# A decoder trunk in fp32 on one core: the first modulation partly as raw fp32 products on TensorE, and four weight units loaded as wide rows

## Chip, core and metric

The kernel runs on one core of one Trainium2 chip. The metric is the device time of one launch in microseconds (us), and the kernel before takes a median of 2716.3 us over three runs. The engines are named as the profile names them: PE is TensorE (PEld its weight loads), DVE is VectorE, ACT is ScalarE, POOL is GpSimd, and SP issues nearly all transfers (DMAs).

## What is computed

Two decoder layers on one sequence of 1024 rows with 1024 columns. Each layer has a token mixer (a gated spatial MLP in layer 0, dilated attention in layer 1) and a dense MLP, and each of these four sub-layers is modulated by a vector c: a shift, a scale and a gate come out of a product of silu(c) with its own weights ada_w.

```python
def ada_mod(c, w, b):
    m = jax.nn.silu(c) @ w + b
    shift, scale, gate = jnp.split(m, 3, axis=-1)
    return shift[:, None, :], scale[:, None, :], 1.0 + gate[:, None, :]

def mixer_a(h, w_in, b_in, vn_g, vn_b, w_s, b_s, w_out):
    uv = jax.nn.gelu(h @ w_in + b_in)
    u, v = jnp.split(uv, 2, axis=-1)
    v = layer_norm(v, vn_g, vn_b)
    ...                                   # z: v mixed over rows within chunks of 128
    return (u * z) @ w_out

# layer i
shift, scale, gate = ada_mod(c, ada_w[i, 0], ada_b[i, 0])
h = x * (1.0 + scale) + shift
y = mixer_a(h, ...)                       # layer 1: mixer_b
x = layer_norm(ALPHA * x + gate * y, ln_g[i, 0], ln_b[i, 0])
...                                       # the same again with squared_relu_mlp
```

All data is fp32. ada_w of one sub-layer has 1024 rows (the index of c) and 3072 columns (shift, scale, gate).

## The kernel before

Every large product is made of three passes with fp32r operands: both factors are cut into a high part (a cast to fp32r) and a low part (the difference), by `split`, and PE adds high times high, high times low and low times high. Left factors stand as 128x128 weights, right factors stream 512 columns. The whole program is unrolled at build time into one fixed instruction list for each engine. A list scheduler sets the order on each engine, except where the code pins an instruction to program order (`tc.keep_in_program_order`). Each engine then runs its list strictly from the front and waits on semaphores.

The change lies in the first stage alone. Until the first modulation is known, no product of the model can run. In the kernel before the stage goes so:

- `c` and a part of ada_b are loaded into `rows_c`, transposed by PE (L79), and silu(c) stands as 8 columns of 128 in `silu_c`.
- `ada_steps` makes the modulation. For each of shift and scale (`part` 0 and 1) and each half of 512 columns (`h`), eight blocks of 128 rows of ada_w (`adaw`, 128x512, 256 KB, L122) are loaded and added up on DVE with silu(c) as the scalar of each partition: one TENSOR_SCALAR (L125) and seven SCALAR_TENSOR_TENSOR (L128) into `adaacc`. Then `adaacc` is split into `adahi` and `adalo`, and PE sums over the partitions: for each of four column blocks two products with `ones_r`, 128x2 (L162, L163, tile `psa`). DVE adds ada_b (L167). `mods(h)` runs shift and scale of one half side by side; up to ten `adaw` tiles are in flight.
- `build_hT` makes h transposed for rows 0 to 511, one block k of 128 columns at a time: four transposes on PE (`pst`, L221), scale and shift on ACT (L226, tile `h`), the cut into `hT` high and low (L102, L103). Blocks 0 to 3 need the first half of the modulation, blocks 4 to 7 the second.
- `v_sum` multiplies `hT` with the weights of v, eight units of 128 output columns. A unit's weights (`winv_raw`, 512 KB) come as 8 blocks of 128x128, that is in pieces of 512 bytes (L353); ACT casts the high part, and for the first four units POOL subtracts the low part (`winv_lo`, `v_unit(G)`). Blocks 0 to 3 are multiplied for units 0 to 3 between the two halves of the modulation, blocks 4 to 7 after them. `v_end` then applies the gelu (L475) and transposes back (`psvt`, L478).
- After that come rows 512 to 1023, the units 4 to 7 of v, the units of u, and the rest of the kernel. The modulations of the later sub-layers run in the background in small steps (`tick`), with the same `ada_steps`.

All loads of this stage stand in one queue on SP in program order. A load waits there until the buffer that it fills is free, and everything behind it waits with it.

## Time and profile before

| | |
|---|---|
| median of three runs | 2716.3 us (2712.53 to 2717.81) |
| the profiled execution's own time | 2717.79 us |
| its span (first to last instruction) | 2716.1 us |
| PE busy in the span | 2655.5 us (98%) |
| first product of a v unit starts (L470) | 25.81 us |
| last product of units 0 to 3 on rows 0 to 511 starts | 60.4 us |
| HBM traffic over the span | 185 GB/s |

A row of the profile's timeline gives the start in us from the span's start, the duration in us, engine, line, operation, output<-inputs, the count of like instructions that were merged, and in brackets how long the engine was idle before and what released it. Durations of merged rows run from the first start to the last end. A row of the table by stretches gives busy us and instruction counts for each engine, the clock that the throttle granted to PE, the DMA share and GB/s.

### The profile page before, as it was taken

The numbers are of one execution on the slowest core, as the hardware profiler recorded it, in microseconds if no ns is written. First come the engines' busy times: TensorE is split into PE (matmuls) and PEld (weight loads), VectorE is DVE, ScalarE is ACT, GpSimd is POOL, SyncE is SP. The second block draws the span as 40 slices with busy tenths as digits, with TensorE's granted clock in tenths as the row PEclk, the third lists the DMA queues.
The fourth block names the chain that finished last, engine by engine and source line by source line (L and its number), as shares of the span: only waits on it lengthen the run. The fifth ranks groups of instructions, "written<-read, shape, count | busy, mean of one in ns | idle before, by whom it ended". The sixth has DMA issues, their size and how long they took to land.

```text
span 2716.1 us, 37099 instructions
## 1 busy us (share of the span) xinstructions
PE 2655.5 (98%) x13242; PEld 2193.5 (81%) x13242; DVE 1993.0 (73%) x3610; ACT 1378.4 (51%) x2601; POOL 114.9 (4%) x193
## 2 busy tenths in 40 slices
PE   6999999999999999999999999999999999999998
PEld 5788887888788878888888888888887888878887
DVE  6787697777889778655647767777658966577877
ACT  3354375555444454433436666666645655544332
POOL 1000000000000001111111000000010000000000
PEclk9999999999999999999999999999999999999999
DMA  7534336667967745655475545554782654495562
GB/s 264 159 118 135 116 137 217 223 223 243 344 229 247 245 148 180 215 179 198 165 225 172 138 133 140 138 146 133 235 219 98 213 190 155 147 317 183 172 208 86
DMA packets 340781, 504.77 MB, mean 186 GB/s; under 512 B 51900, under 2 KB 177252, under 8 KB 340596
## 3 DMA queue, kind: packets, MB, share of 16 engines
q1 hardware_dynamic: 324212, 443.68, 51.5%
q0 software_dynamic: 16384, 58.73, 6.0%
q8 instruction: 104, 1.70, 0.3%
q14 instruction: 81, 0.66, 0.1%
HBM read 365.40 MB, written 136.92 MB: 185 GB/s over the span
## 4 chain that ended last, share of the span: by engine, by line
PE 76%; DVE 12%; DMA 6%; ACT 3%; issue 2%; SPq 0%; DVEq 0%; ACTq 0%
PE psd L957 22%; PE psv L1283 13%; PE psk L1384 6%; PE psq L1384 6%; PE psua L798 6%; DMA adaw<-in_ada_w_dram 3%; PE psd_wout L389 3%; PE pv L1553 3%; PE psuc L798 3%; PE psu L368 3%; PE sc L1473 3%; PE psv L470 2%; DVE adaacc L128 2%; DVE left L103 1%; PE pT L1526 1%
## 5 line engine op out<-in xcount | busy, mean ns | idle before, releaser
L798 PE MATMUL psua<-right,left 128*128 128x512 f32 x1536 | 364.8, 391 | 0.1
L957 PE MATMUL psd<-rhi,lhi 128*128 128x512 f32 x896 | 349.7, 390 | 3.0 <-ACT part L829 3.0
L957 PE MATMUL psd<-rlo,lhi 128*128 128x512 f32 x896 | 349.6, 390 | 0.2
L957 PE MATMUL psd<-rhi,llo 128*128 128x512 f32 x896 | 349.3, 390 | 0.0
L798 PEld LDWEIGHTS psua<-right,left 128*128 128x128 f32 x1536 | 288.3, 188 | 61.6 <-DVE right L103 1.2
L1495 ACT ACTIVATE p<-p,stat 128x128 f32<-128x128 f32 (+1 forms) x384 | 168.8, 441 | 96.8 <-DVE stat L1493 95.8
L957 PEld LDWEIGHTS psd<-rhi,lhi 128*128 128x128 f32 x896 | 168.6, 188 | 39.2 <-ACT part L829 3.9
L957 PEld LDWEIGHTS psd<-rlo,lhi 128*128 128x128 f32 x896 | 168.5, 188 | 35.9 <-DVE rlo L103 1.1
L957 PEld LDWEIGHTS psd<-rhi,llo 128*128 128x128 f32 x896 | 168.6, 188 | 34.9
L798 PE MATMUL psuc<-right,left 128*128 128x512 f32 x768 | 187.2, 390 | 0.0
L128 DVE SCALAR_TENSOR_TENSOR adaacc<-adaw,silu_c,adaacc 128x512 f32<-128x512 f32 x168 | 128.6, 775 | 59.6 <-DMA adaw<-in_ada_w_dram 59.0
L798 PEld LDWEIGHTS psuc<-right,left 128*128 128x128 f32 x768 | 143.6, 188 | 29.9 <-DVE right L103 0.2
L103 DVE TENSOR_TENSOR pTlo<-pT,pThi 128x512 fp32r<-128x512 f32 (+1 forms) x160 | 99.3, 621 | 75.9 <-ACT pThi L102 75.0
L103 DVE TENSOR_TENSOR left<-ws,left 128x512 fp32r<-128x512 f32 x128 | 87.9, 688 | 73.2 <-ACT left L102 71.3
L103 DVE TENSOR_TENSOR llo<-lraw,lhi 128x1024 fp32r<-128x1024 f32 x112 | 136.4, 1218 | 1.5 <-ACT lhi L102 1.5
L102 ACT CAST left<-ws 128x512 fp32r<-128x512 f32 x128 | 79.1, 620 | 104.5 <-DVE ws L719 92.0
L1384 PE MATMUL psk<-form_L,wqk_hi 128*128 128x512 f32 x384 | 126.9, 411 | 0.0
L1384 PE MATMUL psq<-form_L,wqk_hi 128*128 128x512 f32 x384 | 126.4, 410 | 0.0
L102 ACT CAST lhi<-lraw 128x1024 fp32r<-128x1024 f32 x112 | 117.3, 1047 | 9.3 <-PE psd L957 3.3
L1283 PE MATMUL psv<-vrhi,form_S 128*128 128x512 f32 x384 | 120.0, 391 | 1.3 <-DVE vpart L1249 0.8
L1493 DVE CUSTOM_DVE_ANT_0 p<-sc,bias 128x128 f32<-128x128 f32 (+1 forms) x384 | 113.7, 346 | 5.2 <-PE sc L1473 4.9
L102 ACT CAST pThi<-pT 128x512 fp32r<-128x512 f32 (+1 forms) x160 | 84.6, 530 | 60.4 <-PE pT L1526 43.3
(332 smaller groups left out, 6072.3 us busy)
## 6 DMA issues: line engine op xcount, KB each, us to landing
lraw<-forms SPq DMA_DIRECT2D x112, 512.0 KB
adaw<-in_ada_w_dram SPq DMA_DIRECT2D x192, 256.0 KB
up<-in_mlp_w_up_dram SPq DMA_DIRECT2D x64, 512.0 KB
forms<-s SPq DMA_DIRECT2D x128, 256.0 KB
rraw<-in_mlp_w_down_dram SPq DMA_DIRECT2D x64, 512.0 KB
forms<-part SPq DMA_DIRECT2D x96, 256.0 KB
v<-vs POOLq DMA_DIRECT2D x48, 512.0 KB, 3.7
vraw<-in_b_w_qkv_dram SPq DMA_DIRECT2D x42, 512.0 KB
```

The source lines that it names most:

```text
L102: first = A.copy(hi, src) if hi_engine is A else hi_engine.tensor_copy(hi, src)
L103: return first, lo_engine.tensor_tensor(lo, src, hi, op=ALU.subtract)
L128: ins = V.scalar_tensor_tensor(acc[:], raw[:], silu_c[:, k : k + 1], acc[:], ALU.mult, ALU.add)
L368: T.matmul(dst, s[a], m[b], start=(n == 0), stop=(n == last))
L389: T.matmul(p[:], stat[a][:, k, o : o + P], u[b][:, w], start=n == 0, stop=n == count - 1)
L798: T.matmul(acc, w[:, a, k, :], right[p][:, b, k, :], start=p in (1, 2, 5) and k + a + b == 0, stop=k == 3 and a == 1, skip_group_check=True)
L957: ins = T.matmul(sums[kind, m][:], l[a][:, k, m * P : (m + 1) * P], r[b][:, k, :], start=p in (1, 5, 2, 3) and kp + k + a + b == 0, stop=k ...
L1283: T.matmul(acc, rows[:, m * P : (m + 1) * P], cols_, start=p in (1, 2, 5) and kp + k + a + b == 0, stop=kp == 1 and k == 1 and a == 1, ski ...
L1384: T.matmul(p[:], wu[a][:, k * P : (k + 1) * P], h_op(k, half, b), start=k + c_ == 0, stop=k == KD - 1 and c_ == 2)
L1473: T.matmul(banks[e][:, sl], q_[a][rows, tq], k_[b][rows, keys], start=c_ == 0, stop=c_ == 2)
L1493: V.tensor_tensor_reduce(out=pr, in0=banks[e][:, sl], in1=st["bias"][:, width - w :], scale=-0.125, scalar=3e38, op0=ALU.add, op1=ALU.min, ...
L1495: A.activation(pr, pr, AF.Exp, bias=nm, scale=-1.0, accum_out=l)
```

## The change

The first modulation (sub-layer 0, shift and scale) leaves `ada_steps` and gets its own function, `first_mods`. For each half of 512 columns it loads shift and scale together: eight blocks of 128x2x512, 512 KB each, into six buffers. Of the eight blocks the first ones (three for half 0, one for half 1, the list `direct`) are multiplied on PE as they are: eight fp32 products of a 128x128 piece of raw weights with one column of silu(c), added up in one `psa` tile of 8 columns. The other blocks are added up on DVE, shift and scale in one instruction of 1024 columns, the last block in two of 512. Eight fp32 products with a column `one` then add the DVE sum over the partitions to the same `psa` tile, and one DVE instruction adds ada_b. The split of `adaacc` goes. ada_b is loaded after the weights, and 1 is added to its scale part once.

The weights of v units 0 to 3 are loaded as four tiles of 2 blocks of 128 rows by 512 columns (`load_wide`, in pieces of 2048 bytes), and one cast and one subtraction (`cut_wide`) serve two blocks k of all four units. So blocks k are multiplied for four units at a time. In the code, block k of the second modulation is summed behind the products of block k+1.

```diff
+    def first_mods(h, where, direct):
+        w = slice(h * HALF, (h + 1) * HALF)
+        raws, skip = {}, dict(skip_group_check=True)
+        def load(k):
+            raws[k] = where.tile([P, 2, HALF], F32, name=f"adaw_{h}_{k}", tag="adaw", bufs=6)
+            nc.sync.dma_start(raws[k][:], ada_w[0, 0, k * P : (k + 1) * P, 0 : 2 * D].rearrange("p (t c) -> p t c", t=2)[:, :, w])
+        pst, acc = bank("tr", f"psa_{h}"), where.tile([P, 2, HALF], F32, name=f"adaacc_{h}", tag="adaacc")
+        def summed(k):
+            if k in direct:
+                for n in range(8):
+                    ins = T.matmul(pst[:, n : n + 1], raws[k][:, n // 4, (n % 4) * P : (n % 4 + 1) * P], silu_c[:, k : k + 1],
+                                   start=k == direct[0] and n == 0, stop=False, **skip)
+                    if n == 0:
+                        tc.keep_in_program_order(ins)
+                return
+            parts = (1, 0) if k == KD - 1 else (slice(0, 2),)
+            for t in parts:
+                a, src = acc[:, t], raws[k][:, t]
+                if k == len(direct):
+                    ins = V.tensor_scalar(a, src, silu_c[:, k : k + 1], None, ALU.mult)
+                else:
+                    ins = V.scalar_tensor_tensor(a, src, silu_c[:, k : k + 1], a, ALU.mult, ALU.add)
+                tc.keep_in_program_order(ins)
+        def total():
+            mod = cst.tile([P, 2, 4], F32, name=f"mod_{h}")
+            for t in (1, 0):
+                for n in range(4 * t, 4 * t + 4):
+                    T.matmul(pst[:, n : n + 1], acc[:, t, (n % 4) * P : (n % 4 + 1) * P], one[:], start=False, stop=True, **skip)
+            V.tensor_tensor(mod[:], pst[:, 0:8].rearrange("p (t n) -> p t n", t=2),
+                            cols_b[:, 0:16].rearrange("p (t n) -> p t n", t=2)[:, :, 4 * h : 4 * h + 4], op=ALU.add)
+            ada[0]["mul", h], ada[0]["add", h] = mod[:, 1, :], mod[:, 0, :]
...
+                        if u < 4:
+                            w = wide[k // 2][a_][:, k % 2, u * P : (u + 1) * P]
+                        else:
+                            w = units[u][a_][:, k * P : (k + 1) * P]
...
-                groups = ada_steps(0, MODS, ada0, 10)
...
-                mods(0)
-                tiles = [vec.tile([P, D], F32, name=f"x0_{i}", tag=("lng", "lnb")[i]) for i in range(2)]
...
-                        mods(1, ((2, lambda: v_begin(2)), (5, lambda: v_begin(3))))
...
-                        v_unit(G)
-                        v_unit(G)
-                    for k, _ in zip(last_ks if h else first_ks, build_hT(0, 0, tiles, in_pair(hT[0]), last_ks if h else first_ks)):
...
+                def load_wide(kk):
+                    t = wts.tile([P, 2, HALF], F32, name=f"winv_raw_{kk}", tag="raw", bufs=2)
+                    nc.sync.dma_start(t[:], a_w_in[0, 2 * kk * P : 2 * (kk + 1) * P, D : D + HALF].rearrange("(k p) c -> p k c", p=P))
+                    wide_raw.append(t)
+                def cut_wide():
+                    wide.append(tuple(wts.tile([P, 2, HALF], F32R, name=f"winv_{m}_{len(wide)}", tag=f"w{m}") for m in ("hi", "lo")))
+                    hi, lo = wide[-1]
+                    for x_ in split(hi[:], lo[:], wide_raw.popleft()[:], lo_engine=G):
+                        tc.keep_in_program_order(x_)
...
+                (load0, sum0, total0), (load1, sum1, total1) = (first_mods(h, ada0, d) for h, d in ((0, (0, 1, 2)), (1, (0,))))
+                for k in range(KD):
+                    load0(k)
+                rows_b = ada0.tile([64, P], F32, name="rows_b")
+                nc.sync.dma_start(rows_b[:], ada_b.rearrange("i s (q p) -> (i s) q p", p=P)[:, 0 : 2 * KD, :])
+                load_x(0)
+                for kk in range(2):
+                    load_wide(kk)
+                for k in range(KD):
+                    sum0(k)
+                ptb = bank("tr", "rows_bt")
+                tc.keep_in_program_order(T.transpose(ptb[:, 0:64], rows_b[0:64, :], ident[0:64, 0:64]))
+                tc.keep_in_program_order(V.tensor_copy(cols_b, ptb[:, 0:64]))
+                V.tensor_scalar(cols_b[:, KD : 2 * KD], cols_b[:, KD : 2 * KD], 1.0, None, ALU.add)
+                total0()
+                for k in range(KD):
+                    load1(k)
+                load_x(1)
+                for kk in range(2, 4):
+                    load_wide(kk)
+                rows = load_rows()
+                hTs = build_hT(0, 0, tiles, in_pair(hT[0]), range(4))
+                for k in range(4):
+                    if k % 2 == 0:
+                        cut_wide()
+                    next(hTs)
+                    for u in range(4):
+                        v_sum(u, 0, [k])
+                    if k:
+                        sum1(k - 1)
+                run(hTs)
+                for k in range(3, KD):
+                    sum1(k)
+                total1()
+                pt = bank("tr", "rows_t")
+                T.transpose(pt[:, 0:P], rows[:], ident[:])
+                V.tensor_copy(cols[:], pt[:, 0:P])
+                hTs = build_hT(0, 0, tiles, in_pair(hT[0]), range(4, KD))
+                for k in range(4, KD):
+                    if k % 2 == 0:
+                        cut_wide()
+                    next(hTs)
+                    for u in range(4):
+                        v_sum(u, 0, [k])
+                run(hTs)
```

How the instructions move, at three places. Numbers at the ends of names are buffer numbers; `winv_hi` and `winv_lo` are the cut weights of v, `hT_0_0` and `hT_0_1` the high and low part of h for rows 0 to 511, `psv` the sums of the units.

On PE in the kernel before, where the products of unit 1 on blocks 0 to 3 end and those of unit 2 begin, between the two halves of the modulation:

```order
L470 MATMUL psv_0_245<-hT_0_0_129,winv_lo 128x512
L470 MATMUL psv_0_249<-hT_0_0_129,winv_hi 128x512
L470 MATMUL psv_0_249<-hT_0_1_130,winv_hi 128x512
L470 MATMUL psv_0_249<-hT_0_0_129,winv_lo 128x512
L470 MATMUL psv_0_324<-hT_0_0_129,winv_hi 128x512 [waits Activation_49]
L470 MATMUL psv_0_324<-hT_0_1_130,winv_hi 128x512
L470 MATMUL psv_0_324<-hT_0_0_129,winv_lo 128x512 [waits Pool_49]
L470 MATMUL psv_0_324<-hT_0_0_129,winv_hi 128x512
```

On PE now, where the products of blocks 0 and 1 for all four units end:

```order
L509 MATMUL psv_0_266<-hT_0_0_129,winv_hi_241 128x512
L509 MATMUL psv_0_266<-hT_0_1_130,winv_hi_241 128x512
L509 MATMUL psv_0_266<-hT_0_0_129,winv_lo_242 128x512
L196 MATMUL psa_141<-silu_c,adaw_0_212 128x1 [waits DMAHW7_49,PE_49]
L196 MATMUL psa_141<-silu_c,adaw_0_212 128x1 x7
L257 MATMUL pst_0_2_303<-ident,x_136 128x128 [waits PE_49]
L257 MATMUL pst_0_2_303<-ident,x_136 128x128
L257 MATMUL pst_0_2_303<-ident,x_2_137 128x128
L257 MATMUL pst_0_2_303<-ident,x_3_138 128x128
```

Eight products of the second modulation (`psa_141`) now stand on PE behind the 24 products of blocks 0 and 1, and the transposes of blocks 2 and 3 stand behind them.

On DVE in the kernel before, while the second half of the modulation is added up (`adaacc_1_1` for scale, `adaacc_0_1` for shift):

```order
L102 CAST hT_0_0_129<-h_0_1_258 128x512 [waits Activation_49]
L103 TENSOR_TENSOR hT_0_1_130<-h_0_0_241,hT_0_0_129 128x512 [waits Activation_49]
L103 TENSOR_TENSOR hT_0_1_130<-h_0_1_258,hT_0_0_129 128x512 [waits DVE_49]
L128 SCALAR_TENSOR_TENSOR adaacc_1_1_300<-adaw_1_1_1_306,silu_c,adaacc_1_1_300 128x512 [waits DMAHW3_49]
L128 SCALAR_TENSOR_TENSOR adaacc_0_1_304<-adaw_0_1_1_309,silu_c,adaacc_0_1_304 128x512 [waits DMAHW4_49]
L102 CAST hT_0_0_129<-h_0_3_288 128x512 [waits Activation_49]
L103 TENSOR_TENSOR hT_0_1_130<-h_0_2_273,hT_0_0_129 128x512 [waits Activation_49]
L103 TENSOR_TENSOR hT_0_1_130<-h_0_3_288,hT_0_0_129 128x512 [waits DVE_49]
```

On DVE now, in the same part (`adaacc_142` holds shift and scale of half 1):

```order
L102 CAST hT_0_0_129<-h_0_1_275 128x512 [waits Activation_49]
L103 TENSOR_TENSOR hT_0_1_130<-h_0_1_275,hT_0_0_129 128x512 [waits DVE_49]
L103 TENSOR_TENSOR hT_0_1_130<-h_0_2_308,hT_0_0_129 128x512 [waits Activation_49]
L205 TENSOR_SCALAR adaacc_142<-adaw_1_214,silu_c 128x1024 [waits DMAHW0_49]
L102 CAST hT_0_0_129<-h_0_3_330 128x512 [waits Activation_49]
L103 TENSOR_TENSOR hT_0_1_130<-h_0_3_330,hT_0_0_129 128x512 [waits DVE_49]
L207 SCALAR_TENSOR_TENSOR adaacc_142<-adaw_2_216,silu_c,adaacc_142 128x1024 [waits DMAHW1_49]
L207 SCALAR_TENSOR_TENSOR adaacc_142<-adaw_3_218,silu_c,adaacc_142 128x1024 [waits DMAHW2_49,DVE_49]
```

In the kernel before the second modulation's first steps stand among the cuts of blocks 0 to 3. Now its first step stands behind the cut of block 2, and its other steps behind that of block 3.

On DVE in the kernel before, behind the second modulation, where the last blocks of h are cut:

```order
L103 TENSOR_TENSOR hT_0_1_130<-h_0_4_434,hT_0_0_129 128x512 [waits Activation_49]
L102 CAST hT_0_0_129<-h_0_7_497 128x512 [waits Activation_49]
L103 TENSOR_TENSOR hT_0_1_130<-h_0_7_497,hT_0_0_129 128x512 [waits DVE_49]
L103 TENSOR_TENSOR hT_0_1_130<-h_0_6_476,hT_0_0_129 128x512 [waits Activation_49]
L125 TENSOR_SCALAR adaacc_2_0_905<-adaw_2_0_0_903,silu_c 128x512 [waits DMAHW1_49]
L128 SCALAR_TENSOR_TENSOR adaacc_2_0_905<-adaw_2_0_1_907,silu_c,adaacc_2_0_905 128x512 [waits DMAHW2_49,DVE_49]
L479 COPY vz<-psvt_0_515 128x4x128 [waits PE_49]
```

On DVE now, at the same place:

```order
L103 TENSOR_TENSOR hT_0_1_130<-h_0_4_375,hT_0_0_129 128x512 [waits Activation_49]
L102 CAST hT_0_0_129<-h_0_5_396 128x512 [waits Activation_49]
L103 TENSOR_TENSOR hT_0_1_130<-h_0_5_396,hT_0_0_129 128x512 [waits DVE_49]
L125 TENSOR_SCALAR adaacc_2_0_850<-adaw_2_0_0_848,silu_c 128x512 [waits DMAHW5_49]
L128 SCALAR_TENSOR_TENSOR adaacc_2_0_850<-adaw_2_0_1_852,silu_c,adaacc_2_0_850 128x512 [waits DMAHW6_49,DVE_49]
L102 CAST hT_0_0_129<-h_0_7_442 128x512 [waits Activation_49]
L103 TENSOR_TENSOR hT_0_1_130<-h_0_7_442,hT_0_0_129 128x512 [waits DVE_49]
L103 TENSOR_TENSOR hT_0_1_130<-h_0_6_421,hT_0_0_129 128x512 [waits Activation_49]
```

The first two steps of a later modulation's gate (`adaacc_2_0`) stood behind the cut of the last block, and now stand ahead of it. On SP the loads keep the order of the code: half 0, ada_b, x, two wide tiles, half 1, x, two wide tiles, the small rows, x of rows 512 to 1023. The load of block 6 of half 1 waits there for the eight products on PE shown above, and that of block 7 for DVE's first step on `adaacc_142`.

More of the change, by code (lines that the diff above doesn't have):

```diff
@@ L67, in trunk @@
     silu_c = cst.tile([P, KD], F32, name="silu_c")
+    one = cst.tile([P, 1], F32, name="one")
     with ExitStack() as first:
@@ L170, in total @@
                     sh, sc = ada[j][0, h], ada[j][1, h]
[L171 to L180 removed]
+                    mul = cst.tile([P, 4], F32, name=f"mul_{j}_{h}")
@@ L182, in ada_steps @@
+                    add = cst.tile([P, 4], F32, name=f"add_{j}_{h}")
+                    o = slice(4 * h, 4 * h + 4)
+                    V.tensor_tensor(mul[:], g_col(j - 1)[:, o], sc[:], op=ALU.mult)
+                    V.tensor_tensor(add[:], b_col(j - 1)[:, o], sc[:], op=ALU.mult)
+                    V.tensor_tensor(add[:], add[:], sh[:], op=ALU.add)
+                    ada[j]["mul", h], ada[j]["add", h] = mul, add
             todo.append([lambda k=k, step=step: step(k) for k in range(KD)] + [bias_row, reduce, total])
@@ L183, in ada_steps @@
         return todo
+    def first_mods(h, where, direct):
[29 more added lines that the diff above has]
+            ada[0]["mul", h], ada[0]["add", h] = mod[:, 1, :], mod[:, 0, :]
+        return load, summed, total
@@ L457, in mixer_a, with v_unit @@
             hT = [act_pair(f"hT_0_{half}") for half in range(2)]
-            units, sums = [], {}
-            def v_unit(lo_engine=V):
-                u = len(units)
-                units.append(unit(a_w_in[0, :, D + u * P : D + (u + 1) * P], f"winv_{u}", lo_engine=lo_engine))
+            units, wide, sums = {}, [], {}
+            def v_unit(u):
+                units[u] = unit(a_w_in[0, :, D + u * P : D + (u + 1) * P], f"winv_{u}")
             def v_sum(u, half, ks):
@@ new lines, in cut_wide, with load_rows @@
+                def cut_wide():
[3 more added lines that the diff above has]
+                        tc.keep_in_program_order(x_)
+                def load_rows():
+                    rows = work.tile([P, P], F32, name="rows", tag="h")
+                    V.memset(rows[:], 0.0)
+                    nc.sync.dma_start(rows[o_g : o_g + n_ln, :], ln_g.rearrange("i s (k p) -> (i s k) p", p=P))
+                    nc.sync.dma_start(rows[o_b : o_b + n_ln, :], ln_b.rearrange("i s (k p) -> (i s k) p", p=P))
+                    nc.sync.dma_start(rows[o_s : o_s + 16, :], a_b_s.rearrange("l g t -> (l g) t"))
+                    nc.sync.dma_start(rows[o_i : o_i + 2 * KD, :], a_b_in.rearrange("l (k p) -> (l k) p", p=P))
+                    return rows
@@ L555, in mixer_a @@
                 for u in range(4, KD):
[L556 removed]
+                    v_unit(u)
                     for half in range(2):
```

57 lines of the change are left out of this document (12 added, 45 removed).

## Prediction

> **What bounds the kernel now.** I read the page's busy times first, then the table by stretches of 10 us, then the chain of waits and the timeline of the first 62 us, where the whole change lies.
>
> ```profile
> PE 2655.5 (98%) x13242; PEld 2193.5 (81%) x13242; DVE 1993.0 (73%) x3610; ACT 1378.4 (51%) x2601; POOL 114.9 (4%) x193
> core 0: us, PE busy (x) PEld busy (x) DVE busy (x) ACT busy (x) POOL busy (x), PEclk, DMA share, GB/s
> 0.00:10.00 10.00, 0.45 (x1) 0.18 (x1) 4.21 (x12) 1.49 (x2) 0.70 (x6) 1.00 0.67 213
> 10.00:20.00 10.00, 0.96 (x5) 0.88 (x5) 8.71 (x13) 1.24 (x2) 0.00 (x0) 1.00 1.07 385
> 20.00:30.00 10.00, 9.24 (x37) 8.06 (x37) 6.96 (x12) 6.33 (x9) 4.86 (x2) 1.00 1.04 360
> ...
> 40.00:50.00 10.00, 6.93 (x40) 6.23 (x39) 6.64 (x14) 3.33 (x6) 0.00 (x0) 0.83 0.62 218
> ...
> 80.00:90.00 10.00, 8.84 (x46) 7.28 (x45) 6.91 (x12) 3.09 (x5) 0.00 (x0) 1.00 0.48 150
> ```
>
> PE is idle for 60.6 us of the span (2716.1 less 2655.5). The first 20 us hold 18.6 of them, and 40 to 50 us another 3.1. So PE sets the end, and the stage that the change touches is the one place where it waits long. Behind this stage PE is nearly always busy and the lists are fixed. A shift of the stage's end is therefore carried to the end of the kernel, less what later waits of PE take up.
>
> The stage is two waits, one for each half of the modulation:
>
> ```profile
> 14.61 4.10 DVE L128 SCALAR_TENSOR_TENSOR adaacc<-adaw,silu_c,adaacc 128x512 f32<-128x512 f32 x6 [1.27 <-DMA adaw<-in_ada_w_dram]
> 23.28 0.16 DVE L167 SCALAR_TENSOR_TENSOR ada<-psa,cols_c 128x4 f32<-128x4 f32 x1 [1.67 <-PE psa L163]
> 25.81 1.22 PE L470 MATMUL psv<-hT,winv_hi 128*128 128x512 f32 x2
> 31.12 12.28 DVE L128 SCALAR_TENSOR_TENSOR adaacc<-adaw,silu_c,adaacc 128x512 f32<-128x512 f32 x12
> 40.45 0.39 PE L470 MATMUL psv<-hT,winv_lo 128*128 128x512 f32 x1
> 46.05 0.16 DVE L167 SCALAR_TENSOR_TENSOR ada<-psa,cols_c 128x4 f32<-128x4 f32 x1 [0.73 <-PE psa L163]
> 49.55 9.24 PE psv L470 x39
> 58.93 1.21 issue
> ```
>
> Half 0 is summed on DVE at 18.7 us, is known at 23.4, and lets the first v product start at 25.8. Half 1 is summed at 43.4, known at 46.2, and PE, out of work since 40.8, goes on with products at 49.2. Units 0 to 3 end near 60.7.
>
> **The prices.** These rows give what one instruction takes:
>
> ```profile
> 19.99 0.35 PE L162 MATMUL psa<-ones_r,adahi 128*128 128x2 f32 x1
> 20.20 0.35 PE L163 MATMUL psa<-ones_r,adalo 128*128 128x2 f32 x1
> 44.42 0.25 PE L163 MATMUL psa<-ones_r,adalo 128*128 128x2 f32 x1
> 44.53 0.25 PE L162 MATMUL psa<-ones_r,adahi 128*128 128x2 f32 x1
> 28.38 0.63 PE L470 MATMUL psv<-hT,winv_lo 128*128 128x512 f32 x1
> 28.80 0.63 PE L470 MATMUL psv<-hT,winv_hi 128*128 128x512 f32 x1
> 35.55 0.39 PE L470 MATMUL psv<-hT,winv_lo 128*128 128x512 f32 x1
> 36.23 0.39 PE L470 MATMUL psv<-hT,winv_lo 128*128 128x512 f32 x1
> 23.10 3.03 PE L221 MATMUL pst<-ident,x 128*128 128x128 f32 x13
> 5.56 0.88 DVE L125 TENSOR_SCALAR adaacc<-adaw,silu_c 128x512 f32<-128x512 f32 x2
> L103 DVE TENSOR_TENSOR llo<-lraw,lhi 128x1024 fp32r<-128x1024 f32 x112 | 136.4, 1218 | 1.5 <-ACT lhi L102 1.5
> 23.62 1.63 ACT L226 ACTIVATE h<-pst,ada,ada 128x512 f32<-128x512 f32 x2 [0.55 <-PE pst L221]
> 25.15 0.61 ACT L102 CAST hT<-h 128x512 fp32r<-128x512 f32 x1
> 20.53 1.04 ACT L102 CAST winv_hi<-winv_raw 128x1024 fp32r<-128x1024 f32 x1 [1.17 <-DMA winv_raw<-in_a_w_in_dram]
> 21.65 4.86 POOL L103 TENSOR_TENSOR winv_lo<-winv_raw,winv_hi 128x1024 fp32r<-128x1024 f32 x2 [20.27 <-ACT winv_hi L102]
> 27.05 1.28 DVE L103 TENSOR_TENSOR hT<-h,hT 128x512 fp32r<-128x512 f32 x2
> ```
>
> PE runs at two paces. A narrow product with its weight load follows the last one by 0.21 us at the start and by 0.11 later. A 512-column product takes 0.43 at the start and 0.23 later (two thirds of a 0.68 us step over three). The change of pace came at about 32.3 us, after 4.5 us of dense 512-column products. A transpose takes about 0.21 slow. DVE's STT of 512 columns costs 0.68 (4.10 over 6). Of 1024 columns none is in the trace: at least the 1.22 of a subtraction of that width, at most twice 0.68. I take 1.3, since the fixed part is paid once. A 512 KB load lasts 1.36 us at 385 GB/s.
>
> The fp32 product of the change is not in the trace either. It holds a 128x128 weight load and one column. In the compiled program each stands as two loads with a product each (high and low part of the weights), so I take 0.43 slow and 0.22 fast, twice the `psa` row, which is nearest: the same load of 128x128 and a column or two. The bounds are one row (0.21, 0.11) and four rows (0.86, 0.43). Nothing in it can be negative, as the weight load is there in any case.
>
> **Half 0.** The x pieces (0.5 MB) no longer go ahead of the last weights, which is 1.4 us, and c is loaded first. The eleventh of 16 pieces landed at 14.6 and five more at 0.68 give 18.0 before; now 16.0, between 15.5 and 16.6. DVE follows with two steps of 512 columns and ends at 17.4. PE's 24 raw products (24 x 0.43 = 10.3 us from 4.8) end at 15.1, ahead of that. They are hidden, and would stand on the path from 0.5 each on. The sum over partitions, 16 narrow products in two casts and cuts before, is 8 fp32 products: 3.4 us from the first half's end at 16.7, so 20.1, and the modulation is known at 20.3. That is 3.1 us gained. Then seven transposes (1.5), ACT for h (0.8) and its cast (0.6). ACT's cast of the wide weights, 1.04, was done ahead of h before and now stands behind it. The first v product starts at 24.0 against 25.8: **1.8 us gained**.
>
> **Between the halves.** Blocks 0 and 1 are 24 products. POOL's low part is ready at 24.0 + 2.4 = 26.4, when five of them are done (a 0.3 us wait). With 11 slow and 13 fast they end at 32.1. Behind them PE has the 8 raw products of half 1 (1.8 fast) and four transposes (0.5), then come h (0.8) and two cuts (1.2): 36.5. Only then does DVE, in program order behind the cut of block 2, begin half 1. DVE has nothing else from 29 to 36 us, though five of the blocks lie in memory. Its steps: 0.9, the cut of block 3 for 1.0, five of 1.3 and two of 0.68, together 9.8, end at **46.4**. Before, the sum was there at 43.4, as its steps ran beside blocks 0 to 3. The path's work did not grow. It was put behind PE.
>
> SP is held as well. The load of block 6 waits for the raw products, to 34, and with it block 7, x, two wide tiles and the small rows: 2.6 MB, 6.8 us at 385 GB/s and about 2.5 us to the first landing, so 46.5 for the last. Needed are the x pieces at 49.5 and the third wide tile at 51. This is hidden with 3 us to spare.
>
> **Half 1 to the end of the stage.** Eight fp32 products at the slow pace, since PE has waited from 41.4 on (the clock was at 0.83 on average in 40 to 50 us before, too): 45.8 + 3.4 = 49.2, known at 49.4 against 46.2. Then a transpose of the rows and 11 of x (2.5): products from 52.1 against 49.2. Blocks 4 and 5 take 24 products, a few slow: 58.1. The last transposes (0.6) stand behind them, and blocks 6 and 7 need two h and a cast (2.2) after the first of these: PE waits 1.9 and starts again at 60.5. 24 x 0.23 and a wait of 0.3 for the low part give 66.3, against 60.7: **5.6 us lost** at this point.
>
> **What is given back.** PE waits for loads and DVE in the stage behind (1.2 us in 80 to 90 us). A stage that starts later finds these further on, so I give back 1.4. The wide rows (2 MB less in 512-byte pieces; 385 against 360 GB/s in the rows above, 0.4 us) and the small copies on DVE beside the 3.4 us of PE's sums cost or bring nothing, because the queue and DVE are idle there; uncovered they are 0.4 each.
>
> Sum: +5.6 - 1.4 = **+4.2 us**. The profiled execution took 2717.8 (span 2716.1), so it would be 2722.0; against the median of 2716.3 it is **2720.5**. With STT at 1.22 or 1.36 it is 0.5 less or more; with loads at the bounds and the pace changing up to 3.4 us earlier or later, 3 us either way: 2716.5 to 2724.5. About 0.2%, 5.4 us, is what a measurement of this kernel can tell from no change, so this case lies on both sides of that line.
>
> **Rivals.**
>
> *The raw products wake the clock (faster).* 24 products in a row from 4.8 us might bring PE to its fast pace by 9. Then the sums take 1.8 instead of 3.4, seven transposes 0.8, the first 11 products lose 0.2 each, the sums of half 1 a little: 6 us less, 2714.5. With a product at one row on top, 3 us less: 2711.5. Against it: the `psa` products ran from 18.75 to 23.1 at 0.21 to the end. The Trainium skill, TensorE: Matmul & The Clock Gate, Part 1, says that about 3.4 us of sustained activity release the clock; by that rule this rival holds. Here 4.3 us of narrow products did not, so it is not the number of them that counts. 15%.
>
> *Four rows for each product (slower).* At 0.86 block 1's raw products end at 18.6, the load of block 7 waits for that, half 0 is known at 32, and the eight products twice in half 1 add 5 more: +18, 2734. It decides from 0.5 us a product on. The Trainium skill, FP8 and Floating Point Precision, TensorE Precision Notes, counts four passes for true fp32; by that rule the sum is this one if each pass loads its weights again. The compiled two loads and the one column speak against it. 11%.
>
> *The next modulation's load blocks the last cut (slower).* DVE's order now has two gate steps ahead of the cut of block 7.
>
> ```profile
> 50.27 1.30 SPq L122 DMA_DIRECT2D adaw<-in_ada_w_dram  x2
> 57.36 0.49 DVE L125 TENSOR_SCALAR adaacc<-adaw,silu_c 128x512 f32<-128x512 f32 x1 [4.16 <-DMA adaw<-in_ada_w_dram]
> ```
>
> Before, this load took 7.1 us to land, with nothing behind it. Now it stands behind late x loads, landing between 54.6 (3.1 MB at full rate from 46.5) and 61.9 (57.4 and 4.5 us). If it lands after 58.5, each us holds the last 24 products: up to +4, 2724.5. 27%.
>
> **How the numbers follow.** My case has 47%, of which 33 are within 0.2% and 14 slower; the blocked cut 27% (25 slower), four rows 11% (slower), the fast clock 15% (10 faster, 5 within). That makes faster 0.10, same 0.40, slower 0.50. The range goes from 2711.5 to 2730: it leaves out most of the four rows' case and the end of the fast clock's.
>
> **What would show it.** Right: a first v product near 24, DVE idle from 29 to 36 us, half 1 summed near 46.4, PE idle from 41 to 46 and from 58.6 to 60.5, and units 0 to 3 ending near 66. Raw products 0.43 apart show the price. Wrong: raw products at another pace, half 1 summed before 44, or a DMA as what the cut of block 7 waits for.

## The result and the profile after

The changed kernel takes a median of 2725.3 us (2720.2 to 2738.2, 11 runs) against 2715.9 for the kernel before on the same chip (11 runs); the ratio is 1.0041, with a 95% interval of 1.0031 to 1.0052. That is slower by some 11 us. The forecast was 2720.5 in a range of 2711.5 to 2730.

The page of the changed kernel, and its table by stretches of 10 us (columns as before; the third last is the granted clock):

```profile
PE 2668.7 (98%) x13307; PEld 2205.5 (81%) x13307; DVE 1981.8 (73%) x3588; ACT 1376.3 (51%) x2597; POOL 114.2 (4%) x193
```
```profile
30.00:40.00 10.00, 8.87 (x45) 7.37 (x45) 2.60 (x5) 2.17 (x3) 0.00 (x0) 0.90 0.23 71
40.00:50.00 10.00, 7.28 (x33) 6.04 (x32) 8.06 (x8) 0.99 (x1) 0.00 (x0) 0.84 0.99 328
50.00:60.00 10.00, 9.18 (x38) 7.64 (x39) 3.09 (x7) 3.07 (x5) 4.78 (x2) 0.74 0.77 262
```

PE is busy 13 us longer and the span still grows: busy time that was hidden or spent at the slow pace is no gain. In the row from 30 to 40 us DVE works 2.6 us and the DMA engines 0.23 of the time. There nobody is at work on half 1.

The timelines of PE and DVE, and the waits of SP, show why:

```profile
5.48 10.37 PE L196 MATMUL psa<-silu_c,adaw 128*128 128x1 f32 x48 [2.90 <-DMA adaw<-in_ada_w_dram]
17.32 3.58 PE L214 MATMUL psa<-one,adaacc 128*128 128x1 f32 x16 [0.15 <-DVE adaacc L207]
24.95 2.50 PE L509 MATMUL psv<-hT,winv_hi 128*128 128x512 f32 x5 [2.25 <-ACT winv_hi L102]
33.67 1.84 PE L196 MATMUL psa<-silu_c,adaw 128*128 128x1 f32 x16
47.63 2.97 PE L214 MATMUL psa<-one,adaacc 128*128 128x1 f32 x16 [2.72 <-DVE adaacc L207]
51.59 2.55 PE L257 MATMUL pst<-ident,x 128*128 128x128 f32 x11
54.22 1.38 PE L509 MATMUL psv<-hT,winv_hi 128*128 128x512 f32 x3
62.55 1.79 PE L509 MATMUL psv<-hT,winv_hi 128*128 128x512 f32 x5 [1.60 <-ACT hT L102]
68.73 1.23 PE L517 MATMUL psvt<-ident,vt 128*128 128x128 f32 x8
```
```profile
16.51 1.42 DVE L207 SCALAR_TENSOR_TENSOR adaacc<-adaw,silu_c,adaacc 128x512 f32<-128x512 f32 x2 [1.33 <-DMA adaw<-in_ada_w_dram]
37.55 0.69 DVE L103 TENSOR_TENSOR hT<-h,hT 128x512 fp32r<-128x512 f32 x1 [7.13 <-ACT hT L102]
38.16 0.75 DVE L205 TENSOR_SCALAR adaacc<-adaw,silu_c 128x1024 f32<-128x1024 f32 x1
40.22 8.01 DVE L207 SCALAR_TENSOR_TENSOR adaacc<-adaw,silu_c,adaacc 128x1024 f32<-128x1024 f32 x7
59.65 0.75 DVE L128 SCALAR_TENSOR_TENSOR adaacc<-adaw,silu_c,adaacc 128x512 f32<-128x512 f32 x1 [0.23 <-DMA adaw<-in_ada_w_dram]
62.02 0.43 DVE L102 CAST hT<-h 128x512 fp32r<-128x512 f32 x1 [1.62 <-ACT h L262]
```
```profile
SPq L189 <- PE psa L196: 17.2, 3, 10.6
```

The first v product starts 0.9 us earlier than before. Then DVE waits 7.13 us for the cut of block 2, whose h stands behind 24 products and 8 raw products on PE, and begins half 1 at 38.2 though its blocks 0 to 5 have landed. SP waits 17.2 us in all for raw products to free a buffer, 10.6 of them at the load of half 1's block 6. Half 1 is summed at 48.2 (43.4 before), block 4 starts at 54.2 (49.2), and the transposes of `psvt`, which close the stage, at 68.7 (60.9): 7.9 us late.

### The profile page after: what moved, and what is told of

Read it like the earlier page. It is cut to its first block, busy times and chain, and to the rows that moved or that the text cites. A ratio compares the mean times of both kernels' runs of the same rounds, so it can differ in the third digit from the quotient of the medians.

```text
span 2720.0 us, 37160 instructions
## 1 busy us (share of the span) xinstructions
PE 2668.7 (98%) x13307; PEld 2205.5 (81%) x13307; DVE 1981.8 (73%) x3588; ACT 1376.3 (51%) x2597; POOL 114.2 (4%) x193
## 4 chain that ended last, share of the span: by engine, by line
PE 59%; issue 22%; DVE 9%; DMA 6%; POOL 2%; ACT 2%; SPq 0%; POOLq 0%; DVEq 0%; ACTq 0%
PE psd L1032 11%; PE psua L873 8%; PE psk L1459 7%; PE psq L1459 6%; PE psuc L873 4%; PE psu L404 3%; PE psd_wout L425 3%; PE pv L1628 3%; PE sc L1548 3%; DMA adaw<-in_ada_w_dram 3%; PE psv L509 2%; PE psub L873 2%; PE pT L1601 1%; DVE left L103 1%; POOL v L1335 1%
## 5 line engine op out<-in xcount | busy, mean ns | idle before, releaser
L1032 PEld LDWEIGHTS psd<-rhi,lhi 128*128 128x128 f32 x896 | 168.2, 188 | 38.9 <-ACT part L904 3.9
L128 DVE SCALAR_TENSOR_TENSOR adaacc<-adaw,silu_c,adaacc 128x512 f32<-128x512 f32 x140 | 105.1, 751 | 58.2 <-DMA adaw<-in_ada_w_dram 57.4
```

The lines of the kernel that those rows point to most:

```text
L128: ins = V.scalar_tensor_tensor(acc[:], raw[:], silu_c[:, k : k + 1], acc[:], ALU.mult, ALU.add)
L1032: ins = T.matmul(sums[kind, m][:], l[a][:, k, m * P : (m + 1) * P], r[b][:, k, :], start=p in (1, 5, 2, 3) and kp + k + a + b == 0, stop=k ...
```

## Experiments

Ten further runs were made in three groups, each group on one chip and with its own measurements of the kernel before. A marker further on is ACT's table load near 303 us, the same instruction in all kernels. Half 1's sum, block 4's first product and the first `psvt` are read from the timelines, in us.

| kernel | half 1 summed | block 4 | stage's end | marker | ratio to before (95%) |
|---|---|---|---|---|---|
| before, second trace | 43.4 | 49.2 | 60.8 | 303.0 | 0.9989 (0.9980 to 0.9998) |
| change | 48.2 | 54.2 | 68.7 | 311.8 | 1.0041 (1.0031 to 1.0052) |
| change again | 47.9 | 53.6 | 69.1 | 310.7 | 1.0040 (1.0026 to 1.0054) |
| steps early | 43.8 | 49.3 | 67.6 | 309.7 | 1.0026 (1.0014 to 1.0037) |
| half 0 all on DVE | 46.6 | 52.3 | 64.1 | 307.1 | 1.0037 (1.0024 to 1.0050) |
| half 1 all on DVE | 43.9 | 49.2 | 64.2 | 306.6 | 1.0017 (1.0009 to 1.0026) |
| both on DVE | 40.9 | 47.0 | 61.5 | 304.3 | 1.0018 (1.0009 to 1.0026) |
| wait filled | 48.4 | 53.2 | 68.1 | 310.3 | 1.0031 (1.0020 to 1.0043) |
| narrow pieces | 48.0 | 53.7 | 68.9 | 310.8 | 1.0037 (1.0025 to 1.0049) |
| interleaved | 39.4 | 45.7 | 60.8 | 303.1 | 1.0009 (1.0000 to 1.0019) |
| rows earlier | 38.9 | 43.9 | 57.7 | 300.4 | 0.9995 (0.9983 to 1.0007) |

The kernel before against itself gives 0.9989, so a ratio can be off by 0.001 beside its interval. Differences below that are not used.

**Steps early** (order alone).

```diff
-                    if k:
-                        sum1(k - 1)
+                    if k == 1:
+                        for j in range(0, 6):
+                            sum1(j)
                 run(hTs)
-                for k in range(3, KD):
+                for k in range(6, KD):
                     sum1(k)
```

> Only the calls of half 1's steps stand earlier (blocks 0 to 5 behind block 1's products instead of one per block behind blocks 1 to 3); DVE then has the first three of its seven steps ahead of the cut of block 2. Theory A (the order holds half 1 behind PE's progress): those three steps run between 30 and 36 us instead of after 38, half 1 is summed at 41.5 to 44 instead of 48.2, the first product of block 4 starts at 48 to 50.5 instead of 54.2, and the time falls by 4 to 6 us, to about 2720. Rival B (the 8 raw products of half 1, which stand late on PE and keep the load of block 6 back until 35.5 us, are what costs): the sum still ends at 46 or later, since the last two blocks land no earlier, and the time stays within 2 us of 2725. Rival C (the loss lies in a lower granted clock in later stages, not here): the start of block 4 moves but the time does not.

DVE, PE and the table by stretches of this kernel:

```profile
29.87 0.74 DVE L205 TENSOR_SCALAR adaacc<-adaw,silu_c 128x1024 f32<-128x1024 f32 x1
30.64 2.60 DVE L207 SCALAR_TENSOR_TENSOR adaacc<-adaw,silu_c,adaacc 128x1024 f32<-128x1024 f32 x2
37.15 0.69 DVE L103 TENSOR_TENSOR hT<-h,hT 128x512 fp32r<-128x512 f32 x1 [3.90 <-ACT hT L102]
```
```profile
46.94 0.30 PE L592 MATMUL rows_t<-ident,rows 128*128 128x128 f32 x1 [1.79 <-DMA rows<-in_a_b_in_dram]
49.25 1.65 PE L509 MATMUL psv<-hT,winv_hi 128*128 128x512 f32 x3 [0.55 <-ACT hT L102]
67.56 1.23 PE L517 MATMUL psvt<-ident,vt 128*128 128x128 f32 x8
```
```profile
50.00:60.00 10.00, 8.39 (x30) 6.59 (x29) 2.96 (x6) 2.76 (x4) 2.40 (x1) 0.76 0.59 189
60.00:70.00 10.00, 9.64 (x39) 6.90 (x39) 4.06 (x7) 3.81 (x5) 0.00 (x0) 0.83 0.59 181
```

The first two DVE rows fill 3.3 of the idle 7 us, 3.9 remain, and block 4 starts 5.0 us earlier: theory A holds for the wait. B's bound (sum at 46 or later) is missed. But from block 4 to the stage's end this kernel needs 18.3 us where the change needs 14.5: the granted clock is 0.76 and 0.83 while PE works through the last 48 products, and the stage ends only 1.2 us earlier. The ratio falls by 0.0015, some 4 us, but the two intervals overlap. So in this trace most of the wait that was cut short was repaid in the clock, a case that none of the three theories had.

**Raw products off in half 0, in half 1, in both.** The list of raw blocks is emptied (and the sums over partitions then start their columns):

```diff
-... for h, d in ((0, (0, 1, 2)), (1, (0,))))
+... for h, d in ((0, ()), (1, (0,))))          # half 0
+... for h, d in ((0, (0, 1, 2)), (1, ())))     # half 1
+... for h, d in ((0, ()), (1, ())))            # both
```

> Half 0 without raw products: all eight blocks on DVE; half 1 and all orders as in the change. The prediction held the three raw blocks of half 0 to be hidden and half 0 bound by its loads. DVE needs 0.75 + 6 x 1.30 + 2 x 0.70 = 10 us from 5.5 us on, and frees its buffers at 1.3 us a block where the raw products free them at 3.4. If that is right the load of block 7 goes out before 9 us instead of at 12.5, half 0 is summed at 16 to 18 (now 17.9), the first v product starts at 24 to 25.5 (now 24.95), and the time stays within 2 us of 2725. If instead the raw products are what gains the 1 us at the start, the sum moves to 19 or later and the time rises by 1 to 3 us.

> Half 1 without raw products: all eight blocks on DVE; half 0 and the places of the calls as in the change. The first DVE step then stands ahead of the cut of block 2 and releases the load of block 6 at about 30 us instead of 35.5; PE loses 1.8 us of raw products between blocks 1 and 2. Theory A (order): the other seven steps still stand behind the cut of block 2, which comes 1.8 us earlier, so the sum ends at 44 to 46.5 and the first product of block 4 at 50 to 52; time 2 to 4 us below 2725. Rival B (raw products): the sum ends at 42 to 43.5, block 4 starts at 48 to 49.5, time 5 to 7 us below, better than with the early steps alone. Rival C (later clock): time unmoved.

> No raw products in either half, calls where the change has them. If the two halves' raw products act on separate waits, the result is the sum of the two single removals. Theory A: first v product at 24 to 25.5, half 1 summed at 43 to 46, block 4 from 49 to 51.5, time 2720 to 2723. Rival B: block 4 from 47 to 49, time 2715 to 2719, level with the kernel before or better. Rival C: 2723 or more.

PE of half 0 all on DVE, then PE of half 1 all on DVE, with DVE's first step on half 1:

```profile
16.08 1.86 PE L214 MATMUL psa<-one,adaacc 128*128 128x1 f32 x8 [3.05 <-DVE adaacc L207]
22.81 2.07 PE L509 MATMUL psv<-hT,winv_hi 128*128 128x512 f32 x4 [1.47 <-ACT hT L102]
48.97 3.62 PE L257 MATMUL pst<-ident,x 128*128 128x128 f32 x16
64.13 1.24 PE L517 MATMUL psvt<-ident,vt 128*128 128x128 f32 x8
```
```profile
43.40 2.75 PE L214 MATMUL psa<-one,adaacc 128*128 128x1 f32 x16 [3.67 <-DVE adaacc L207]
49.21 1.65 PE L509 MATMUL psv<-hT,winv_hi 128*128 128x512 f32 x3
64.17 1.23 PE L517 MATMUL psvt<-ident,vt 128*128 128x128 f32 x8
31.37 0.74 DVE L205 TENSOR_SCALAR adaacc<-adaw,silu_c 128x1024 f32<-128x1024 f32 x1
```

Without its raw products half 0 is known sooner, and the first v product starts at 22.8, 2.1 us ahead of the change and 1.2 ahead of what was expected. The three raw blocks were not hidden: each held its buffer for 3.4 us, so the load of block 7 went out at 12.5 instead of 7.9 us. Half 0 is known 0.9 us sooner (20.2 against 21.1); the rest of the 2.1 comes from ACT's wait for the transposes of block 0, which ends 0.4 us after that here and 1.4 us after it in the change. The other 2.5 us at the stage's end are no merit of that: the scheduler put all 16 transposes of blocks 4 to 7 ahead, and the wait that the change has at 62.5 is gone. In the ratio this kernel can't be told from the change; its runs spread from 2716.9 to 2733.1.

Half 1 without raw products brings block 4 forward by 5.0 us and the time by about 6.5 (1.0041 to 1.0017). The sum came at 43.9, just ahead of A's 44 to 46.5 and behind B's 42 to 43.5; block 4 and the time came as B said. With both off the stage ends 7.2 us earlier (4.6 and 4.5 with one of them off), 0.7 us behind the kernel before. Block 4 came as B said, but the ratio is that of half 1 alone, not level with the kernel before. So nearly the whole delay of the stage goes with the raw products: on PE, where eight of them stand ahead of the transposes for the cut that DVE waits for, and in the buffers that SP waits for. Order and raw products are not taken apart by these runs: without raw products DVE's first step on half 1 runs at 31.4, ahead of the cut of block 2, and steps early brings block 4 to 49.3 with all raw products kept.

**The change again; a filled wait.** The first is the changed kernel once more. In the second 12 products of 512 columns, read by nobody, stand ahead of `total1()`:

```diff
+                fill = bank("tr", "fill")
+                for n in range(12):
+                    tc.keep_in_program_order(T.matmul(fill[:], wide[0][0][:, 0, 0:P], hT[0][0][:, 0, :], start=True, stop=True))
                 total1()
```

> The changed kernel once more, on the chip of this group, for a ratio beside the others and a second trace. If the loss is the stage's delay (7.4 us in the traces at 300 us) and half clocks in the stage, its first 75 us repeat: first v product at 24.5 to 26, half 1 summed at 47 to 49, units 0 to 3 ending at 67.5 to 69, ratio 1.003 to 1.005. If most of the rest comes from half-clock stretches that fall anywhere behind the stage, this trace shows them at other places or in another number than the first, and single times differ by about their sum.

> The changed kernel with 12 more products of 512 columns (a block that lies in memory, into an unused bank, read by nobody) on PE between the products of block 3 and the sum over partitions of half 1, where PE waits 2.7 us. Theory D (part of the loss is the slow pace that PE falls into because it waits there): the products cost nothing, since 12 x 0.23 = 2.7 us fit the wait; the two half-clock stretches at 38 and 48 to 55 us go or become one, the eight fp32 products of half 1 take 1.9 instead of 3.0 us, the 12 transposes behind them 1.4 instead of 2.6, block 4 starts at 51 to 52.5 instead of 54.2, and the time falls by 2 to 4 us (ratio 1.0025 to 1.0035). If the pace does not depend on it, block 4 starts at 54 to 55.5 and the ratio stays at 1.004 or above.

PE of the change again, then of the filled wait:

```profile
47.30 3.57 PE L214 MATMUL psa<-one,adaacc 128*128 128x1 f32 x16 [4.35 <-DVE adaacc L207]
50.98 2.56 PE L257 MATMUL pst<-ident,x 128*128 128x128 f32 x11
```
```profile
47.82 1.95 PE L214 MATMUL psa<-one,adaacc 128*128 128x1 f32 x16
51.01 2.00 PE L257 MATMUL pst<-ident,x 128*128 128x128 f32 x11
53.17 1.65 PE L509 MATMUL psv<-hT,winv_hi 128*128 128x512 f32 x3 [0.17 <-ACT hT L102]
```

The change repeats within 0.6 us up to block 4. With the wait filled the fp32 sums keep the fast pace (1.95 against 2.97 and 3.57 us), the transposes half of it, and block 4 starts at 53.2, short of the 51 to 52.5 expected. The stage gains 0.6 to 1.0 us. The ratio, 1.0031, is lower by 0.001, which the intervals don't separate: D is right in its mechanism and small in its price, since the clock fell again behind the next wait, 1.1 us for the rows (a share of 0.83 from 50 to 60 us).

**Narrow pieces.** Each wide tile comes as four strips of 128 columns:

```diff
-                    nc.sync.dma_start(t[:], a_w_in[0, 2 * kk * P : 2 * (kk + 1) * P, D : D + HALF].rearrange("(k p) c -> p k c", p=P))
+                    for u in range(4):
+                        nc.sync.dma_start(t[:, :, u * P : (u + 1) * P], a_w_in[0, 2 * kk * P : 2 * (kk + 1) * P, D + u * P : D + (u + 1) * P].rearrange("(k p) c -> p k c", p=P))
```

> The changed kernel with the four wide tiles loaded in four strips of 128 columns each (pieces of 512 bytes, 12 more transfers on SP's queue) into the same tiles; all else as in the change. The prediction gave the wide rows nothing or 0.4 us. Then the time stays within 1 us of the changed kernel's (ratio 1.0035 to 1.005) and the first product of block 4 within 1 us of 54.2. If the piece size matters, the first wide tile lands late, the first v product starts at 26 us or later, and the ratio is 1.005 or more.

First v product at 25.3, block 4 at 53.7, ratio 1.0037: the pieces' size moves nothing here, as forecast.

**Interleaved, then rows earlier.** All blocks on DVE; half 1's steps are pinned between the cuts of blocks 1 to 3; ACT takes their casts; the small rows get a buffer of their own. The second kernel also loads these rows ahead of the last wide tile.

```diff
-            A.activation(h[:], pst[:], AF.Identity, bias=add[:, k % 4 : k % 4 + 1], scale=mul[:, k % 4 : k % 4 + 1])
+            ins = [A.activation(h[:], pst[:], AF.Identity, bias=add[:, k % 4 : k % 4 + 1], scale=mul[:, k % 4 : k % 4 + 1])]
             hi, lo = place(k)
-            split(hi, lo, h[:], hi_engine=V if k % 2 else A)
+            ins += split(hi, lo, h[:], hi_engine=A if cuts == "A" or k % 2 == 0 else V)
+            if cuts:
+                for x_ in ins[2:]:
+                    tc.keep_in_program_order(x_)
...
                     next(hTs)
+                    for j in range(*((0, 0), (0, 2), (2, 4), (4, 6))[k]):
+                        sum1(j)
...
-                    rows = work.tile([P, P], F32, name="rows", tag="h")
+                    rows = ada0.tile([P, P], F32, name="rows")
```

> All blocks of both halves on DVE; half 1's steps stand between the cuts of blocks 1 to 3 and are held there; the cast of the odd blocks 1 and 3 is ACT's instead of DVE's, and the small rows do not share a buffer with h. Theory A with B (order and raw products together, nothing else): half 1 summed at 39 to 41.5, block 4 from 44 to 46.5, units 0 to 3 ended at 57 to 60 (60.8 before), so 1 to 3 us ahead of the kernel before in the trace at 300 us; ratio 0.998 to 1.001. If the rest of the loss (all DVE is level with the kernel before in the trace at 300 us and still 1.0018) belongs to later half-clock stretches, the ratio may stay at 1.001 to 1.002 with the stage ahead.

> As the interleaved kernel, with the four small loads of rows ahead of the last wide tile instead of behind it. There PE waited 2.0 us for these rows ahead of the transposes of x for block 4, and lost its pace in it. The rows land about 1.4 us earlier (512 KB at 385 GB/s), so the transposes start at 41 to 41.7 instead of 42.8, block 4 at 43 to 44.7 instead of 45.7, and units 0 to 3 end at 58.5 to 60 instead of 60.8; ratio 1.000 to 1.001 where the interleaved kernel had 1.0009. If the rows were not what PE waited for, nothing moves.

PE of the first, then of the second:

```profile
38.87 1.92 PE L214 MATMUL psa<-one,adaacc 128*128 128x1 f32 x16 [1.88 <-DVE adaacc L207]
42.81 0.45 PE L594 MATMUL rows_t<-ident,rows 128*128 128x128 f32 x1 [2.02 <-DMA rows<-in_a_b_in_dram]
43.05 2.55 PE L257 MATMUL pst<-ident,x 128*128 128x128 f32 x11
```
```profile
41.05 0.43 PE L594 MATMUL rows_t<-ident,rows 128*128 128x128 f32 x1 [0.75 <-DMA rows<-in_a_b_in_dram]
43.91 1.23 PE L512 MATMUL psv<-hT,winv_hi 128*128 128x512 f32 x3
```

Half 1 is summed at 39.4, 9 us sooner than in the change, and block 4 starts at 45.7, both as expected, but units 0 to 3 end at 60.8 where 57 to 60 were expected. What is late next is a transfer of 8 KB: PE waits 2.02 us for the small rows, with the transposes of x behind it. Loaded earlier, they cost 0.75 us, block 4 starts at 43.9, and the stage ends 3.1 us ahead of the kernel before. Yet the ratios are 1.0009 and 0.9995: level with the kernel before, not ahead of it. None of these versions is clearly faster than the kernel before.

**The kernel before again.**

> The kernel before, unchanged, for a second trace of it and a ratio against itself (1.000, interval within 0.001 of it). Open is a surplus: in the traces the kernels with no raw products (level at 300 us) and with interleaved steps (1.3 us ahead) should be level or faster, but measure 1.0018 and 1.0009. If the first trace of the kernel before was an unlucky one (its profiled run took 2717.8 where the chips of these groups give 2710 to 2712), the second differs from it: units 0 to 3 end 2 to 4 us ahead of 60.8 us, or fewer half-clock stretches than four ahead of the last one. If its first 75 us repeat within 0.5 us and the half-clock stretches are as many, the surplus of the others lies behind 300 us and comes from elsewhere.

The first 75 us repeat within 0.1 us, so the stage's times stand. But the half-clock stretches do not. The next rows are the waits of PE for the sum of a later modulation, in the timelines of the first trace of before, of its second, of the change, of rows earlier and of the change again, with ACT's marker where it is used below; behind them stands the table's stretch from 410 to 440 us of the first trace, of rows earlier and of the change again:

```profile
422.78 0.27 PE L162 MATMUL psa<-ones_r,adahi 128*128 128x2 f32 x1 [2.00 <-ACT adahi L102]
```
```profile
303.04 1.28 ACT L236 ACT_TABLE_LOAD   x1
420.24 0.27 PE L162 MATMUL psa<-ones_r,adahi 128*128 128x2 f32 x1 [0.84 <-ACT adahi L102]
```
```profile
311.82 1.28 ACT L272 ACT_TABLE_LOAD   x1
429.64 0.27 PE L162 MATMUL psa<-ones_r,adahi 128*128 128x2 f32 x1 [1.46 <-ACT adahi L102]
```
```profile
300.37 1.28 ACT L275 ACT_TABLE_LOAD   x1
418.58 0.27 PE L162 MATMUL psa<-ones_r,adahi 128*128 128x2 f32 x1 [1.86 <-ACT adahi L102]
```
```profile
428.97 0.27 PE L162 MATMUL psa<-ones_r,adahi 128*128 128x2 f32 x1 [1.95 <-ACT adahi L102]
```
```profile
410.00:440.00 30.00, 28.00 (x121) 22.82 (x120) 25.30 (x44) 15.39 (x27) 0.00 (x0) 0.94 0.67 220
```
```profile
410.00:440.00 30.00, 28.14 (x114) 22.96 (x113) 23.43 (x41) 15.73 (x28) 0.00 (x0) 0.89 0.63 210
```
```profile
410.00:440.00 30.00, 28.05 (x128) 23.01 (x127) 25.42 (x44) 16.91 (x31) 0.00 (x0) 1.00 0.70 229
```

In the twelve traces PE waits between 0.84 and 2.00 us for this sum, in no order with how early it comes there. Behind the waits of 2.00 and 1.86 us the granted clock over these 30 us is 0.94 and 0.89, that is 3.4 and 6.8 us at half clock. Behind 0.84 and 1.46 it stayed full, but so it did behind the 1.95 us of the change again; the length of the wait alone doesn't decide it. In its trace the kernel that leads by 2.7 us at the marker has spent the lead here: 1.0 us of longer wait, and about half of the 6.8. Over all runs of their group the mean granted clock was 0.9958 for the interleaved kernel and 0.9966 for before, which on 2711 us is 2.2 us, about its whole surplus. But some of that lies in the stage, whose time is level already: from 40 to 50 us the clock is 0.66 in the interleaved trace and 0.83 in before, a stretch more, 1.7 us. So the clock explains the surplus only in part. Why such stretches are more frequent behind 300 us in some kernels than in others was not settled; single traces show them at 425, 505, 680, 2040 and 2400 us, not in all kernels at the same ones.

## Why the prediction was right and where it failed

It named the direction with 0.50, the mechanism of the second half, and a range that held the time. The most likely time was 5 us too low. That the range held is partly luck: the band of the forecast's own case, 2716.5 to 2724.5, ends short of 2725.3, and the room above it was left for the rival of four rows, which did not come about.

- **Prices.** 48 loads and products in 10.37 us are 0.432 for each of the 24 fp32 products, and 0.23 at the fast pace (1.84 over 8): 0.43 and 0.22 were forecast. The wide STT took 1.28, forecast 1.3.
- **Half 0.** The first v product came at 24.95, not 24.0. Half 0 was known at 21.1 instead of 20.3; ACT's cast of the wide weights behind h cost its full 1.04, as counted. "They are hidden" was wrong as a claim on the raw products: half 0 all on DVE starts 2.1 us earlier. The landing of the last block was forecast for 16.0 from the rate of the loads, and DVE went on with it at 16.5; but what set it was the buffer that the raw products held until 12.5, so that this term came out near is luck.
- **Between the halves.** The reading "the path's work was put behind PE" held: DVE idle for 7.1 us where 7 were forecast, raw products 1.84 (1.8), half 1's eight steps 10.1 us in all with the cut between them (9.8). Half 1 was summed at 48.2 instead of 46.4, because blocks 0 and 1 began 1 us late and ended at 33.7 instead of 32.1.
- **Half 1 to the stage's end.** Block 4 at 54.2 (52.1), the wait before the last 24 products 1.6 (1.9), the end 7.9 us late (5.6 by the forecast's own count). "Hidden with 3 us to spare" was wrong for the loads behind block 6: the small rows, forecast to land at 46.5, came at 51.3, and PE waited 0.75 us for them. (The 34, 6.8 and 2.5 us that the forecast names add up to 43.3; its 46.5 needs the load of block 7 to wait for DVE's first step as well.)
- **What is given back: this step failed.** It took 1.4 us off. Against the second trace of before the marker at 303 us stands 8.8 and 7.6 us late in the two traces of the change, and the end 10.2 and 10.1 us (spans of 2709.8 against 2720.0 and 2719.9). Nothing came back; 1 to 2 us were added behind the stage. These traces come from different chips, but the medians on one chip agree: 2720.7 for the change again, 2710.1 for before. The sum was also made on a trace of before from the slow end: its execution took 2717.8 where the 11 runs beside the change have a median of 2715.9, and it has the half-clock stretch behind 422 us in it. Against that span of 2716.1 the change looks only 3.9 us slower.

So +4.2 became +11: 2.3 in the stage, 1.4 that was not given back, some 1.5 added later, and the rest is what the interval leaves open. The mean granted clock points the same way: 0.9949 over the runs of the change again against 0.9966 for before in the same group, 4.6 us on 2711. In the traces 3.4 of them lie in the stage (three half-clock stretches there against one), which leaves 1.2 behind it.

**The rivals.** *The raw products wake the clock*: no. All 48 ran 0.21 apart for 10.4 us, and the 16 behind them 0.22. The Trainium skill, TensorE: Matmul & The Clock Gate, Part 1, lets about 3.4 us of sustained activity release the clock; the trace does not bear that out for narrow products with their weight loads, 10.4 us of which left the slow pace as it was. The first dense products of 512 columns changed pace 6.4 us after their start (rows of 0.63 us until 30.2, the first of 0.40 at 31.4). *Four rows for each product*: no, two. *The next modulation's load blocks the last cut*: no, its step ended at 60.4, and the cut at 62.0 waited 1.62 us for h.

## What to carry to other kernels

Before work is moved to an idle engine, ask which buffer it holds and for how long: the raw products took work off DVE that DVE does about as fast as the loads come (1.28 us a block against 1.36), and held each 512 KB buffer 3.4 us instead of 1.3, so the next loads and the other half waited. In an engine's fixed list, steps that could run early must not stand behind a step that waits for another engine; look for an idle row whose releaser has nothing to do with the work behind it. And a gain ahead of later waits is only worth what those waits leave of it, so measure it at a marker behind them, against more than one trace of the kernel before.

## What the runs showed of the hardware

A short wait of PE can cost more than its length, for behind some waits the granted clock falls to half. It did so behind waits of 2.00 us (the first trace of before, near 422 us), 1.86 us (rows earlier) and 1.16 us (half 1 all on DVE), and did not behind 1.95 us (the change again) or 2.62 us (half 0 all on DVE, near 563 us). One wait of 1.5 us near 680 us stands in all twelve traces; five of them have a half-clock stretch right behind it, seven have none. So these runs give no length from which a wait costs a stretch.

The stretches last 3.4 us, and two or three can follow each other: shares of 0.83 and 0.66 over 10 us are one and two of them, and in steps of 1 us the clock reads 0.50 inside and 1.00 outside. The Trainium skill, TensorE: Matmul & The Clock Gate, Part 1, states such windows, free-running and of 3.4 us, at half or full rate; the traces agree. The same kernel gets them at different places: the change has shares of 0.90, 0.84 and 0.74 from 30 to 60 us in one trace and 1.00, 0.83 and 0.66 in the other, three stretches in both. Each costs half its length, 1.7 us. With one trace of each kernel, differences of 2 to 5 us in 2710 are within that.

The slow pace at the start does not show in this column. It reads 1.00 from 0 to 30 us in both kernels, while narrow products stand 0.21 us apart and products of 512 columns 0.43. There the pace has to be read from the rows.
